# Splits, sums and scans moved from GpSimd to VectorE in a streaming encoder layer

## The chip, the cores and the metric

The kernel runs on one core of a Trainium2 chip. A core has engines that each work through their own queue of instructions in order: TensorE (PE, with its weight loads as PEld), VectorE (DVE), ScalarE (ACT), GpSimd (POOL) and SyncE (SP), which here issues the loads and stores. They wait for each other by semaphores. The metric is device time in microseconds (us); lower is better.

## What is computed

One layer of an encoder for two groups of tokens that share all weights, 512 tokens of a prompt and 32 of a sample (with cached keys, values and states). Everything is float32. Cut to what matters:

```
mod = silu(c) @ w_ada + b_ada;  sh1, sc1, g1, sh2, sc2, g2 = split(mod)
h   = layer_norm(x) * (1 + sc1) + sh1
a_q, a_k, a_v, m_qk, m_v, m_if, m_o = split(h @ w_in)
a_out = differential attention, 4 heads: softmax - lam * softmax, block-causal mask
m_out = mLSTM, 4 heads: conv on q/k, gates, cumulative sum and running maximum over tokens
y_a = head_norm(a_out) @ w_br_a;  y_b = head_norm(m_out) * sigmoid(m_o) @ w_br_b
g_a, g_b = split(sigmoid(h @ w_gate + b_gate))
mix = (g_a * y_a + g_b * y_b) @ w_o
x   = layer_norm(ALPHA * x + (1 + g1) * mix)
h2  = layer_norm(x) * (1 + sc2) + sh2
gt, up = split(h2 @ w_gu);  ffn = (silu(gt) * up) @ w_down
y   = layer_norm(ALPHA * x + (1 + g2) * ffn)
```

## The kernel before

Features lie on the 128 partitions and the 544 tokens on the free axis, in two halves of 256 and 288 tokens. To keep accuracy with TensorE's fast float format, each large product is made of three: every operand is split into a high part (`hi`, `H`: ScalarE's copy into the rounded format) and a low part (`lo`, `L`: the operand minus its high part), and TensorE adds hi x hi, hi x lo and lo x hi. A weight tile is a block of 1024 input rows by 128 columns, held as 128x1024. For each such tile (`Unit`) ScalarE writes `hi`, another engine subtracts and writes `lo`, and TensorE then runs 8 steps of three matmuls for each half of the tokens. `hi`, `lo` and the raw weights `raw` have two buffers each, so a load of new raw weights starts when the last `lo` from that buffer is done, and a `hi` starts when TensorE has left the buffer two tiles back. PSUM banks come from small rings too (tags `g`, `s`, `x`, `o`): a matmul into a reused bank waits for the engine that read it last.

The order is: load and normalise `x`, modulate it into `hH`/`hL` in five stages while the first columns of `w_in` (q and k) are already multiplied (to about 100 us); the rest of `w_in` with attention and mLSTM work laid between its tiles, four groups of columns with the conditioning products between (to about 290 us); the gates; the two branch products, whose results are summed in `br` and split to `mixH`/`mixL` (to about 480 us); `w_o`, the norm and `h2` (to about 580 us); the two feed-forward products (to about 930 us) and the last norm.

Order is set when the program is written out: side work is kept in small generators, and `Lane` emits their steps between the main stream's matmuls, by cost estimates for ScalarE, VectorE and GpSimd. On each engine the emitted order is the order in which it runs.

Who makes the low parts differs by place. Lines as in the profile: `vtt` (L153) is a VectorE operation on two tensors, `gtt` (L157) the same on GpSimd, `sub2` (L159) gives 3 of the 8 slices to GpSimd and 5 to VectorE. `group_split` (L478) uses `gtt` for the first weights, `hunits(..., gtt)` (L1540) for 22 tiles of `w_in`, `sub2` serves `w_o` and the first part of `w_gu`. `scan32` (L908) runs sums on GpSimd and maxima on VectorE. `rsqrt` (L277) always runs on GpSimd.

Of the kernel before, what the change touches and what calls it, by code (L numbers as in the profile page):

```python
# [9 lines left out]
F32 = mybir.dt.float32  # L10
# [9 lines left out]
T = SEQ + DEC  # L20
# [11 lines left out]


class Lane:
    """Emits the steps of generators between the steps of a main stream, by estimates of when each engine gets there."""

    RATE = {"act": (0.2, 0.83e-3), "dve": (0.13, 1.04e-3), "pool": (0.2, 1.8e-3)}
    LAG = 0.15
# [55 lines left out]
def trunk_kernel(ctx: ExitStack, tc: tile.TileContext, I: dict, O: list):  # L94
    nc = tc.nc
# [10 lines left out]
    lane = Lane()  # L106
# [2 lines left out]
        return sp.tile(shape, dt, tag=f"S{i}", name=name)  # L109

    class Halves:
        """Eight tiles of features by tokens, held in the two halves of a slot."""

        def __init__(self, i, dt, name):
            self.h = [slot(f"{i}{c}", [128, 4, T], dt, f"{name}{c}") for c in "ab"]
# [41 lines left out]
        nc.gpsimd.tensor_tensor(out=out, in0=in0, in1=in1, op=op)  # L157
        lane.op("pool", out)

    def sub2(out, in0, in1, op):  # L160
        gtt(out[:, 0:3], in0[:, 0:3], in1[:, 0:3], op)
        c = lane.chain
        lane.begin()
        vtt(out[:, 3:8], in0[:, 3:8], in1[:, 3:8], op)
        lane.chain = max(c, lane.chain)

    def bns(out, in_):
        nc.vector.bn_stats(out=out, in_=in_)  # L168
# [45 lines left out]
    w_in = I["w_in"][0]  # L214
# [127 lines left out]
    ORDER0 = "0p0c1c1wwg0gg21grgr2ghrhhh3hr2r3hr3hrammh"  # L342

    def rows_stats(mv):
        """Mean and variance of the sample's tokens, each held as four rows of a quarter of its features."""
        c = small([128, 4], "rows_c", 2)
        ps = bank("o", "cmb")
        mm(ps[:, 0:2], quart, mv)
        yield ROWS_WAIT
        vcopy(c[:, 0:2], ps[:, 0:2])  # L350
        vtt(c[:, 2:3], mv[:, 0:1], c[:, 0:1], SUB)
        vtt(c[:, 2:3], c[:, 2:3], c[:, 2:3], MUL)
        yield ROWS_WAIT
        mm(ps[:, 2:3], quart, c[:, 2:3])
        yield ROWS_WAIT
        vtt(c[:, 1:2], c[:, 1:2], ps[:, 2:3], ADD)
        return c
# [56 lines left out]
    hH, hL = Halves(0, F32R, "hH"), Halves(1, F32R, "hL")  # L414

    def modulate(k, part=None):
        """Features of tile k: all tokens, or those of one half."""
        t = tmp([128, T], "mod_t")
        cut = (0, T) if part is None else (HALF[part][0], sum(HALF[part]))
        for a, b, r in ((0, 512, 0), (512, 544, 1)):  # L420
            a, b = max(a, cut[0]), min(b, cut[1])
            if a < b:
                vts(t[:, a:b], xT(k)[:, a:b], modT[:, 8 + k, r:r + 1], modT[:, k, r:r + 1], MUL, ADD)
        c = slice(*cut)
        act(hH(k)[:, c], t[:, c], AF.Copy)
        yield 0
        (vtt if part != 0 else gtt)(hL(k)[:, c], t[:, c], hH(k)[:, c].bitcast(F32), SUB)

    def all_of(gen):
        for _ in gen:  # L430
# [50 lines left out]
    def group_split(x):  # L481
        if x in parts or x >= len(groups):
            return
        s, i = groups[x]
        n = STAGES[s]
        r = w_raw[s][:, i]
        hi = wp.tile([128, 2, 512], F32R, tag="hi", name="hi", bufs=2)
        lo = wp.tile([128, 2, 512], F32R, tag="lo", name="lo", bufs=2)
        act(hi[:, 0:n], r, AF.Copy)
        gtt(lo[:, 0:n], r, hi[:, 0:n].bitcast(F32), SUB)  # L490
        parts[x] = (hi, lo)

    qk_holder = {}
# [75 lines left out]
        return hi, lo  # L569

    class Unit:
        """One n-tile of a product: its weights' parts, its matmuls, what takes its results."""

        def __init__(self, chunk, c0, nk, aH, aL, evac, k0=0, ak0=0, halves=(0, 1), split=None, pss=None,
                     first=True, last=True, need=None, eng=None, late=False):
# [33 lines left out]
                    self.evac(ps, hf, o, n)  # L609

    class IfUnit:
        """The gates' eight columns: the weights' two parts side by side, so that each half of h passes once."""

        chunk, need = None, None

# [107 lines left out]


    def to_tok(src, name, tag="x", part=(0, 1)):
        """[128, T] features by tokens into PSUM as tokens by features: the prompt's four tiles, the sample's."""
        out = []
        for i in part:
            p = bank(tag, name + str(i))
            if i == 0:  # L730
                for tt in range(4):
                    tr(p[:, tt * 128:(tt + 1) * 128], src[:, tt * 128:(tt + 1) * 128], 128)
                out.append(p.rearrange("p (t f) -> p t f", t=4))
            else:
                tr(p[0:32, 0:128], src[:, 512:544], 128)
                out.append(p[0:32, 0:128])
        return out
# [168 lines left out]
        return mv[0:32, 4, h, 0:128] if s else mv[:, 0:4, h, 0:128]  # L906

    def scan32(cur, pp, op):  # L908
        big = gtt if op == ADD else vtt
        for i, s in enumerate((1, 2, 4, 8, 16)):  # L910
            nxt = pp[i % 2].rearrange("p (a b) -> p a b", a=17)
            vcopy(nxt[:, :, 0:s], cur[:, :, 0:s])
            big(nxt[:, :, s:32], cur[:, :, s:32], cur[:, :, 0:32 - s], op)
            cur = nxt
            yield 0
        c = small([4, 16], "scan_c")
        vcopy(c.unsqueeze(2), cur[:, 0:16, 31:32])
        for s in (1, 2, 4, 8):
            d = small([4, 16], "scan_d")
            vcopy(d[:, 0:s], c[:, 0:s])  # L920
            vtt(d[:, s:16], c[:, s:16], c[:, 0:16 - s], op)
            c = d
        vtt(cur[:, 1:16, :], cur[:, 1:16, :], c[:, 0:15].unsqueeze(2).to_broadcast([4, 15, 32]), op)
        yield 0
# [612 lines left out]
    units.append(IfUnit())  # L1537

    for c in range(4):
        units += hunits(w_in, 1536 + c * 256, [conv_evac(2 * c), conv_evac(2 * c + 1)], gtt)  # L1540
        units.append(ada_rest.pop(0))
        d = c % 2
        if c < 2:
            units += hunits(w_in, 2560 + d * 256, [v_evac(2 * d, mv_dst, None), v_evac(2 * d + 1, mv_dst, None)], gtt)
        else:
            units += hunits(w_in, 3080 + d * 256, [og_evac(2 * d), og_evac(2 * d + 1)], gtt)
        units.append(ada_rest.pop(0))

    tas = []
# [34 lines left out]
    def br_b_evac(n):  # L1584
        def f(ps, hf, o, w):
            if not mix:
                mix["H"], mix["L"] = Halves(0, F32R, "mixH"), Halves(1, F32R, "mixL")
            p = tmp([128, 288], "br")[:, 0:w]
            stt(p, tas[1](n)[:, o:o + w], 1.0, ps[:, 0:w], ADD, MUL)
            gtt(p, p, tas[0](n)[:, o:o + w], ADD)  # L1590
            dH, dL = mix["H"](n)[:, o:o + w], mix["L"](n)[:, o:o + w]

            def g():
                act(dH, p, AF.Copy)
                yield 0
                vtt(dL, p, dH.bitcast(F32), SUB)
            mix_tasks.append(lane.add(g()))
        return f
# [152 lines left out]
    def h2_parts(tf, H, L, i):  # L1751
        lane.begin()
        act(H, tf, AF.Copy)
        yield 0
        (gtt if i in POOL_LO else vtt)(L, tf, H.bitcast(F32), SUB)

    def mod2(out, in_, kk, r, eng):
        sc, sh = modT[:, 32 + kk, r:r + 1], modT[:, 24 + kk, r:r + 1]
# [76 lines left out]
            )  # L1835

    SLACK, ROWS_LATE = 2.5, 0.0
    MODE = ((0, 1), (0, 1), (2, 1), (0, 1))
    ACT_MOD = ((0, 2), (0, 1, 3))
    POOL_LO = ((0, 1), (1, 1))  # L1840
    ACT_POOL = ((0, 0), (1, 0))

    wo = {}

# [16 lines left out]
    def split_to(raw, where):  # L1861
        hi, lo = part_pair(where)
        act(hi, raw, AF.Copy)
        sub2(lo, raw, hi.bitcast(F32), SUB)
        return hi, lo

    wo_parts = {}
# [46 lines left out]
    def u_evac(n):  # L1914
        def f(ps, hf, o, w):
# [4 lines left out]
            def g():  # L1920
                act(dH, th, AF.Copy)
                yield 0
                (gtt if (n, hf) in ACT_POOL else vtt)(dL, th, dH.bitcast(F32), SUB)
            act_tasks.append((n, lane.add(g())))
        return f

# [184 lines left out]
```

## Time and profile before

| what | value |
|---|---|
| median of 3 runs | 963.54 us (962.74 to 964.62) |
| profiled execution, first to last instruction | 966.0 us, 2.5 above the median of the runs |
| mean granted TensorE clock of the profiled execution | 0.982 |
| TensorE busy | 916.9 us, 95% |
| VectorE busy | 525.4 us, 54%, 1113 instructions |
| ScalarE busy | 355.8 us, 37% |
| GpSimd busy | 214.1 us, 22%, 253 instructions |
| GpSimd, full `lo` of `w_in` tiles | 20 of 2415 ns |
| VectorE, full `lo` | 72 of 1224 ns |

All times after the third row are of the profiled execution, and places are given in us from its start. A row of the timeline has start, length, engine, line, operation, output<-inputs and shape, and in brackets how long the engine had been idle and what ended that. The releaser is inferred from semaphores.

### The profile page before, as it was taken

To read this page: it belongs to the slowest core of one execution; us is meant where nothing else is said; L and a number is where in the kernel's file an instruction comes from. 1 tells how busy PE (TensorE), PEld (TensorE's weight loads), DVE (VectorE), ACT (ScalarE), POOL (GpSimd) and SP (SyncE) were. 2 spreads that over 40 slices of the span, in tenths; PEclk is the share of its full clock that TensorE was granted. 3 is DMA by queue.
4 is the path that set the end of the run, shared out by engine and by line. 5 is a ranking of instruction groups with operands and counts; after the bars stand their busy time and mean duration, and the time that the engine had idled before them with its cause. 6 is when DMAs were issued, how large, how long until landed. Compare 5 with 4: busy or idle time off the path is not lost. (4 is left out here: it accounts for less than half of the span.)

```text
span 966.0 us, 17335 instructions
## 1 busy us (share of the span) xinstructions
PE 916.9 (95%) x7184; PEld 868.2 (90%) x7184; DVE 525.4 (54%) x1113; ACT 355.8 (37%) x689; POOL 214.1 (22%) x253
## 2 busy tenths in 40 slices
PE   4799999999999999999999989999999999999993
PEld 4679998798798889899999989999999999999993
DVE  4657567877554444446846886544444443223356
ACT  4511466555542332322434474322222222212241
POOL 4433116332411100101741664200000000000014
PEclk8989999999999999999999999999999999999997
DMA  9904423252244244333911502022222226322302
GB/s 281 337 1 127 147 67 112 88 174 89 88 132 143 93 141 133 93 132 124 309 63 45 192 32 89 1 88 88 89 88 88 88 88 232 123 77 77 121 1 92
DMA packets 92283, 110.43 MB, mean 114 GB/s; under 512 B 3897, under 2 KB 75789, under 8 KB 92205
## 3 DMA queue, kind: packets, MB, share of 16 engines
q1 hardware_dynamic: 91996, 109.27, 34.8%
q8 instruction: 56, 0.92, 0.4%
q14 instruction: 23, 0.18, 0.1%
q10 hardware_dynamic: 208, 0.07, 0.0%
HBM read 102.09 MB, written 7.24 MB: 113 GB/s over the span
## 5 line engine op out<-in xcount | busy, mean ns | idle before, releaser
L153 DVE TENSOR_TENSOR lo<-raw,hi 128x1024 fp32r<-128x1024 f32 (+3 forms) x102 | 112.0, 1098 | 130.4 <-ACT hi L132 125.4
L132 ACT ACTIVATE hi<-raw 128x1024 fp32r<-128x1024 f32 (+2 forms) x124 | 122.1, 984 | 153.1 <-PE dn L600 61.6
L600 PE MATMUL dn<-act,hi 128*128 128x288 f32 (+1 forms) x704 | 135.8, 292 | 0.0
L600 PE MATMUL g<-hHa,hi 128*128 128x288 f32 (+1 forms) x344 | 109.1, 317 | 6.2 <-DVE qka L176 4.7
L600 PEld LDWEIGHTS dn<-act,hi 128*128 128x128 f32 x704 | 110.8, 189 | 0.0
L600 PE MATMUL g<-hHb,hi 128*128 128x256 f32 (+1 forms) x352 | 107.8, 306 | 1.3 <-DVE qka L176 1.3
L600 PE MATMUL g<-h2Ha,lo 128*128 128x288 f32 (+1 forms) x352 | 101.4, 288 | 2.4 <-POOL lo L157 1.5
L600 PE MATMUL dn<-act,lo 128*128 128x288 f32 (+1 forms) x352 | 101.8, 289 | 1.8 <-DVE lo L153 1.8
L600 PE MATMUL g<-h2La,hi 128*128 128x288 f32 (+1 forms) x352 | 101.4, 288 | 1.0 <-DVE h2La L153 1.0
L600 PE MATMUL g<-h2Ha,hi 128*128 128x288 f32 (+1 forms) x352 | 102.1, 290 | 0.0
L600 PE MATMUL g<-hLb,hi 128*128 128x256 f32 (+1 forms) x352 | 101.9, 289 | 0.0
L600 PE MATMUL g<-hLa,hi 128*128 128x288 f32 (+1 forms) x344 | 101.2, 294 | 0.8 <-DVE hLa L153 0.7
L600 PE MATMUL g<-h2Hb,hi 128*128 128x288 f32 (+1 forms) x352 | 101.8, 289 | 0.0
L600 PE MATMUL g<-h2Lb,hi 128*128 128x288 f32 (+1 forms) x352 | 101.5, 288 | 0.1
L600 PE MATMUL g<-hHb,lo 128*128 128x256 f32 (+1 forms) x352 | 101.4, 288 | 0.0
L600 PE MATMUL g<-hHa,lo 128*128 128x288 f32 (+1 forms) x344 | 100.7, 293 | 0.2 <-DVE lo L153 0.2
L600 PE MATMUL g<-h2Hb,lo 128*128 128x288 f32 (+1 forms) x352 | 100.8, 286 | 0.0
L157 POOL TENSOR_TENSOR lo<-raw,hi 128x1024 fp32r<-128x1024 f32 (+2 forms) x30 | 63.6, 2122 | 137.1 <-ACT hi L132 126.5
L600 PEld LDWEIGHTS g<-hHa,hi 128*128 128x128 f32 x344 | 66.0, 192 | 23.0 <-issue 6.2
L280 POOL TENSOR_SCALAR rs__10439<-mv__10423 128x1 f32<-128x1 f32 x1 | 0.2, 190 | 322.4 <-DVE mv__10423 L172 322.4
L600 PEld LDWEIGHTS g<-hHb,hi 128*128 128x128 f32 x352 | 66.7, 190 | 5.3 <-issue 2.7
L600 PEld LDWEIGHTS g<-h2Ha,lo 128*128 128x128 f32 x352 | 66.3, 188 | 3.1 <-POOL lo L157 2.0
(490 smaller groups left out, 2180.4 us busy)
## 6 DMA issues: line engine op xcount, KB each, us to landing
raw<-in_w_gu_dram SPq DMA_DIRECT2D x18, 1024.0 KB, 5.1
raw<-in_w_ada_dram SPq DMA_DIRECT2D x16, 1024.0 KB, 5.2
raw<-in_w_in_dram SPq DMA_DIRECT2D x10, 1024.0 KB
raw<-in_w_gate_dram SPq DMA_DIRECT2D x8, 1024.0 KB, 6.7
raw<-in_w_down_dram SPq DMA_DIRECT2D x8, 1024.0 KB, 5.3
wo<-in_w_o_dram SPq DMA_DIRECT2D x4, 1024.0 KB
rawg<-in_w_gu_dram SPq DMA_DIRECT2D x4, 1024.0 KB
raw<-in_w_down_dram SPq DMA_DIRECT2D x3, 768.0 KB
```

What stands on the lines that cost most here:

```text
L132: nc.scalar.activation(out=out, in_=in_, func=func, **kw)
L153: nc.vector.tensor_tensor(out=out, in0=in0, in1=in1, op=op)
L157: nc.gpsimd.tensor_tensor(out=out, in0=in0, in1=in1, op=op)
L280: nc.gpsimd.tensor_scalar(out=out, in0=in_, scalar1=scale, scalar2=EPS, op0=MUL, op1=ADD)
L600: nc.tensor.matmul(ps[:, 0:n], w[:, self.k0 + k, :], a(self.ak0 + k)[:, o:o + n], start=(self.first and k == 0 and p == 0), stop=(self.las ...
```

## The change

Every split that was on GpSimd, wholly or in part, goes to VectorE; so do the sums of the two branches (`br`) and the additions of the scans. A new helper `ltt` is a VectorE operation that still books its time as GpSimd's in `Lane`, so that most of the emitted order stays as it was; where `vtt` is used instead, the booking changes too. In the norm after `w_o`, token tile 2 is now computed by two VectorE passes like the other tiles, where it had one pass on ScalarE, one on VectorE and one on GpSimd. GpSimd keeps the inverse roots, masks, constants and small copies.

```diff
-    def sub2(out, in0, in1, op):
-        gtt(out[:, 0:3], in0[:, 0:3], in1[:, 0:3], op)
-        c = lane.chain
-        lane.begin()
-        vtt(out[:, 3:8], in0[:, 3:8], in1[:, 3:8], op)
-        lane.chain = max(c, lane.chain)
+    def ltt(out, in0, in1, op):
+
+        nc.vector.tensor_tensor(out=out, in0=in0, in1=in1, op=op)
+        lane.op("pool", out)
...
     def modulate(k, part=None):
-        (vtt if part != 0 else gtt)(hL(k)[:, c], t[:, c], hH(k)[:, c].bitcast(F32), SUB)
+        vtt(hL(k)[:, c], t[:, c], hH(k)[:, c].bitcast(F32), SUB)
...
     def group_split(x):
-        gtt(lo[:, 0:n], r, hi[:, 0:n].bitcast(F32), SUB)
+        ltt(lo[:, 0:n], r, hi[:, 0:n].bitcast(F32), SUB)
...
     def scan32(cur, pp, op):
-        big = gtt if op == ADD else vtt
+        big = ltt if op == ADD else vtt
...
-        units += hunits(w_in, 1536 + c * 256, [conv_evac(2 * c), conv_evac(2 * c + 1)], gtt)
+        units += hunits(w_in, 1536 + c * 256, [conv_evac(2 * c), conv_evac(2 * c + 1)], ltt)
...
     def br_b_evac(n):
-            gtt(p, p, tas[0](n)[:, o:o + w], ADD)
+            ltt(p, p, tas[0](n)[:, o:o + w], ADD)
...
     def h2_parts(tf, H, L, i):
-        (gtt if i in POOL_LO else vtt)(L, tf, H.bitcast(F32), SUB)
+        vtt(L, tf, H.bitcast(F32), SUB)
...
-    MODE = ((0, 1), (0, 1), (2, 1), (0, 1))
+    MODE = ((0, 1), (0, 1), (0, 1), (0, 1))
-    POOL_LO = ((0, 1), (1, 1))
-    ACT_POOL = ((0, 0), (1, 0))
...
     def split_to(raw, where):
-        sub2(lo, raw, hi.bitcast(F32), SUB)
+        vtt(lo, raw, hi.bitcast(F32), SUB)
...
-                (gtt if (n, hf) in ACT_POOL else vtt)(dL, th, dH.bitcast(F32), SUB)
+                vtt(dL, th, dH.bitcast(F32), SUB)
```

The edit is made the same way on the other `hunits(..., gtt)` lines. Three places show what it does to the queues. The first is VectorE's queue around 33 us: `mod_t` and `hLa` are the modulated tile and its low part, `s_a` a buffer of raw weights. Before:

```order
L149 TENSOR_SCALAR mod_t<-xTa,modT 128x512
L149 TENSOR_SCALAR mod_t<-xTa,modT 128x32
L153 TENSOR_TENSOR hLa<-mod_t,hHa 128x544
L176 SCALAR_TENSOR_TENSOR qkb<-g,qkb 128x256 x3
L180 COPY gs<-ga 128x512
```

Now:

```order
L149 TENSOR_SCALAR mod_t<-xTa,modT 128x512
L149 TENSOR_SCALAR mod_t<-xTa,modT 128x32
L162 TENSOR_TENSOR lo<-s_a,hi 128x512
L153 TENSOR_TENSOR hLa<-mod_t,hHa 128x544
L174 SCALAR_TENSOR_TENSOR qkb<-g,qkb 128x256 x3
L178 COPY gs<-ga 128x512
L174 SCALAR_TENSOR_TENSOR qkb<-g,qkb 128x256
L162 TENSOR_TENSOR lo<-s_a,hi 128x1024
```

A `lo` stands ahead of `hLa`, and another ahead of the next `qka`; before, both were in GpSimd's queue. The second place is TensorE's queue at about 182 us, with what each row waits for (`v_tok` and `gt` are transposes into banks of the same ring, `gt` of the conditioning sums `ada_gs`). Before:

```order
L600 MATMUL g<-hHa,lo 128x256
L142 MATMUL v_tok_2204<-ident,vT 32x128 [waits DVE_49]
L142 MATMUL gt<-ident,ada_gs 128x128 [waits DVE_49]
L142 MATMUL gt<-ident,ada_gs 128x128 x3
L600 MATMUL g<-hHb,hi 128x256
```

Now:

```order
L598 MATMUL g<-hHa,lo 128x256
L142 MATMUL v_tok_2204<-ident,vT 32x128 [waits DVE_49]
L142 MATMUL gt<-ident,ada_gs 128x128 [waits Activation_49]
L142 MATMUL gt<-ident,ada_gs 128x128 x3
L598 MATMUL g<-hHb,hi 128x256
```

The rows are the same, but `gt` is given another bank of its ring and waits for ScalarE in place of VectorE: for `wT`, ScalarE's copy of transposed attention weights. At about 218 us VectorE's queue changes as in the first place: a `lo` comes in ahead of `colT`, which copies transposed mLSTM rows out of PSUM. The third is VectorE's queue near 578 us, at the last pieces of `h2` (`128x4x32` is the sample's part). Before:

```order
L153 TENSOR_TENSOR h2La<-h2t,h2Ha 128x2x256
L153 TENSOR_TENSOR h2Lb<-h2t,h2Hb 128x2x256
L176 SCALAR_TENSOR_TENSOR th<-th,g 128x256
L153 TENSOR_TENSOR lo<-raw,hi 128x640
L153 TENSOR_TENSOR h2La<-h2t,h2Ha 128x4x32
L153 TENSOR_TENSOR h2Lb<-h2t,h2Hb 128x2x256
```

Now:

```order
L153 TENSOR_TENSOR h2Lb<-h2t,h2Hb 128x2x256
L153 TENSOR_TENSOR th<-th,g 128x256
L153 TENSOR_TENSOR lo<-raw,hi 128x1024
L153 TENSOR_TENSOR h2Lb<-h2t,h2Hb 128x2x256
L153 TENSOR_TENSOR act_6716<-th,act_6715 128x256
L153 TENSOR_TENSOR h2La<-h2t,h2Ha 128x4x32
L153 TENSOR_TENSOR h2Lb<-h2t,h2Hb 128x4x32
```

The `lo` ahead of the sample's `h2La` is now that of the next tile, and two more rows stand between.

More of the change, by code (lines that the diff above doesn't have):

```diff
@@ L1543, in trunk_kernel @@
         if c < 2:
-            units += hunits(w_in, 2560 + d * 256, [v_evac(2 * d, mv_dst, None), v_evac(2 * d + 1, mv_dst, None)], gtt)
+            units += hunits(w_in, 2560 + d * 256, [v_evac(2 * d, mv_dst, None), v_evac(2 * d + 1, mv_dst, None)], ltt)
         else:
-            units += hunits(w_in, 3080 + d * 256, [og_evac(2 * d), og_evac(2 * d + 1)], gtt)
+            units += hunits(w_in, 3080 + d * 256, [og_evac(2 * d), og_evac(2 * d + 1)], ltt)
         units.append(ada_rest.pop(0))
```

## The prediction

> **What bounds the kernel now.** I read the engine totals first, then the table of stretches, then the list of what TensorE waited for.
>
> ```profile
> PE 916.9 (95%) x7184; PEld 868.2 (90%) x7184; DVE 525.4 (54%) x1113; ACT 355.8 (37%) x689; POOL 214.1 (22%) x253
> ```
>
> TensorE is busy for 95% of the span, VectorE for 54%, GpSimd for 22%. So work that moves between the two costs nothing by its sum; it costs or gains only where TensorE waits. In the stretches below the columns are the length, then busy time of PE, PEld, DVE, ACT and POOL with their counts, the granted clock, the DMA share and GB/s.
>
> ```profile
> 48.00:52.00 4.00, 3.32 (x13) 2.88 (x13) 2.20 (x3) 1.29 (x2) 4.00 (x3) 0.50 0.00 2
> ...
> 156.00:160.00 4.00, 4.00 (x21) 3.84 (x22) 3.87 (x10) 1.21 (x5) 0.71 (x1) 0.63 0.56 195
> ...
> 624.00:912.00 288.00, 288.00 (x2300) 288.00 (x2298) 105.51 (x162) 78.81 (x128) 0.00 (x0) 1.00 0.32 104
> ```
>
> From 624 to 912 us TensorE never pauses and GpSimd has no instruction: the change moves nothing there. What it moves lies ahead of 624 us, apart from an untouched tail. The first two rows show something a busy share hides: a few us after a stall the clock fell to 0.50 and 0.63, so a stall can cost more than its length. TensorE's waits (us in total, times, longest):
>
> ```profile
> PE g L600 <- DVE qka L176: 6.0, 3, 3.5
> ...
> PE s_ps L1111 <- DVE mx L992: 1.6, 2, 1.5
> ...
> PE g L600 <- POOL lo L157: 1.5, 1, 1.5
> ...
> PE wT_ps L142 <- DVE ada_gs L153: 1.2, 1, 1.2
> ...
> PE o_ps L136 <- ACT wT L132: 1.1, 1, 1.1
> ...
> PE g L600 <- DVE h2La L153: 1.0, 1, 1.0
> ...
> PE ps_wc L136 <- DVE s_m L180: 0.9, 1, 0.9
> ```
>
> These sum to 13.3 us, and all but the o_ps one end on VectorE or GpSimd. They are most of what the change can win; what it can lose is not in this list, because those waits don't exist yet.
>
> **The price of the moved work.** The groups by form give both engines' times for one operation (count, then busy us and mean ns of one).
>
> ```profile
> L157 POOL TENSOR_TENSOR lo<-raw,hi 128x1024 fp32r<-128x1024 f32 x20 | 48.3, 2415 | 121.4 <-ACT hi L132 111.7 <-ACT lsum L132 9.1 <-DVE s_g L180 0.5
> ...
> L157 POOL TENSOR_TENSOR lo<-rawg,hi 128x384 fp32r<-128x384 f32 x16 | 24.0, 1503 | 19.1 <-ACT hi L132 19.1
> ...
> L157 POOL TENSOR_TENSOR br<-br,ta0a 128x288 f32<-128x288 f32 x4 | 5.1, 1272 | 2.9 <-ACT hi L132 2.0 <-DVE br L176 0.8
> ...
> L153 DVE TENSOR_TENSOR lo<-raw,hi 128x1024 fp32r<-128x1024 f32 x72 | 88.2, 1224 | 95.0 <-ACT hi L132 91.1 <-PE qk_ps L136 3.7
> ...
> L153 DVE TENSOR_TENSOR lo<-rawg,hi 128x640 fp32r<-128x640 f32 x16 | 15.2, 951 | 5.3 <-ACT hi L132 5.3
> ```
>
> A full `lo` takes 2.42 us on GpSimd and 1.22 us on VectorE. The 22 full ones cost VectorE 22 x 1.22 = 27 us; the 32 that it shared go from 640 to 1024 elements, 32 x (1.22 - 0.95) = 9 us or a little more; the 16 `br` sums and the scans add some 10 by the same rate. That is 45 to 55 us more asked of VectorE. Tile 2's normalisation adds one pass over 1024 elements and takes one from ScalarE. All of this is costed at nothing by its length, because TensorE's own work covers it wherever VectorE has idle time; what it costs without that cover is the third rival. VectorE also gets time back, since operations of its own that meet a GpSimd tensor operation take far longer than their size:
>
> ```profile
> 42.05 3.99 DVE L149 TENSOR_SCALAR mod_t<-xTa,modT 128x512 f32<-128x512 f32 x4
> ...
> 42.06 2.35 POOL L157 TENSOR_TENSOR lo<-s_a,hi 128x1024 fp32r<-128x1024 f32 x1
> ```
>
> Two pieces of 512 and two of 32 elements took 3.99 us, 2.35 of them beside the `lo`. [...]
>
> The GpSimd `lo` row shows the other side: it idled 121.4 us before those twenty, 111.7 of it until ScalarE's `hi` was there. GpSimd could afford to stand and wait. VectorE is a queue as well, and now that `lo` stands in it; everything listed behind waits for the same `hi`. So each term below is this (rows of the timeline: start, length, engine, line, operation, in brackets the idle time before and what ended it): when is `hi` ready, plus 1.22 us, plus what stands between, against when TensorE took the result before.
>
> **First stage, 33 to 52 us.**
>
> ```profile
> 33.02 0.72 DVE L153 TENSOR_TENSOR hLa<-mod_t,hHa 128x544 fp32r<-128x544 f32 x1 [0.72 <-ACT hHa L132]
> ...
> 33.77 0.64 ACT L132 ACTIVATE hi<-s_a 128x512 fp32r<-128x512 f32 x1
> ...
> 33.80 0.39 PE L600 MATMUL g<-hLa,hi 128*128 128x256 f32 x1
> ...
> 47.82 1.96 DVE L153 TENSOR_TENSOR hLa<-mod_t,hHa 128x544 fp32r<-128x544 f32 x2
> ...
> 48.24 1.05 ACT L132 ACTIVATE hi<-s_a 128x1024 fp32r<-128x1024 f32 x1
> ...
> 48.59 0.58 PE L600 MATMUL g<-hLa,hi 128*128 128x256 f32 x1 [0.45 <-DVE hLa L153]
> ```
>
> TensorE took `hLa` at 33.80 us, right when it was done. Now a 512 `lo` precedes it, and its `hi` ends at 33.77 + 0.64 = 34.41. With 0.72 us for the `lo` (the 544-element row bounds it) and 0.72 for `hLa`, TensorE goes on at 35.9: **+2.1 us**. Next comes the 3.5 us wait for `qka` at 42.67 to 46.42 us. [...] Then `hLa` again: `hi` ends at 49.29, `lo` at 50.5, `hLa` (half of 1.96, or 0.72) near 51.3 instead of 48.59: **+2.7**.
>
> **142 to 156 us.**
>
> ```profile
> 144.14 0.62 DVE L176 SCALAR_TENSOR_TENSOR s_att<-s_att,r 128x384 f32<-128x384 f32 x1
> ...
> 144.54 1.06 ACT L132 ACTIVATE hi<-raw 128x1024 fp32r<-128x1024 f32 x1 [0.54 <-DMA raw<-in_w_in_dram]
> ...
> 147.20 0.49 PE L142 MATMUL wT_ps<-ident,s_att 128*128 128x128 f32 x3
> ...
> 150.50 5.07 DVE L176 SCALAR_TENSOR_TENSOR cv_y<-cv_u,PT,cv_y 128x547 f32<-128x547 f32 x3
> ```
>
> `s_att` now stands behind that `lo` (ready 145.60, done 146.8) and three `s_g` rows that are no longer than 0.62 each by estimate: done between 147.5 and 149.3 against TensorE's 147.20, so +0.3 to +2.1, I take +1.5. [...]
>
> **182 to 187 us.** Here a wait changes its owner. `gt` got a PSUM bank that VectorE's `s_m` copy released; now it gets the one that ScalarE's `wT` releases (the order rows of TensorE ahead of this text show it).
>
> ```profile
> 178.37 0.37 SPq L184 DMA_DIRECT2D raw<-in_w_in_dram  x1
> ...
> 182.77 0.66 PE L142 MATMUL gt<-ident,ada_gs 128*128 128x128 f32 x4 [0.42 <-DVE s_m L180]
> ...
> 185.17 1.06 ACT L132 ACTIVATE hi<-raw 128x1024 fp32r<-128x1024 f32 x1 [4.17 <-DMA raw<-in_w_in_dram]
> ...
> 186.13 0.47 ACT L132 ACTIVATE wT<-wT_ps 128x384 f32<-128x384 f32 x1
> ```
>
> `wT` waits behind a `hi` that waits for a load, and that load was issued when GpSimd's `lo` left the buffer. VectorE's `lo` leaves it 2.42 - 1.22 = 1.2 us earlier, so `wT` ends at 186.60 - 1.2 = 185.4 and `gt` starts at 185.5 instead of 182.77: +2.7. The o_ps wait of 1.1 for that `wT` is then paid already: **+1.6** (if TensorE were not bound there, -1.1).
>
> **218 us.**
>
> ```profile
> 211.58 0.37 SPq L184 DMA_DIRECT2D raw<-in_w_in_dram  x1
> ...
> 218.41 0.28 PE L142 MATMUL v_tok<-ident,vT 128*32 128x128 f32 x1 [0.21 <-DVE colT L180]
> ...
> 218.78 1.06 ACT L132 ACTIVATE hi<-raw 128x1024 fp32r<-128x1024 f32 x1 [2.53 <-DMA raw<-in_w_in_dram]
> ```
>
> The load takes 7.2 us from issue to `hi`, and comes 0.6 us earlier. `hi` ends at 219.2, `lo` at 220.5, and only then `colT` frees the bank that `v_tok` needs: 220.7 against 218.41, +2.3, less the 0.9 wait of ps_wc just behind: **+1.4**.
>
> **Later places.** [...] The wait for GpSimd's own `lo` at 547 us goes: **-1.5**. Then 578 us:
>
> ```profile
> 578.60 1.06 ACT L132 ACTIVATE hi<-raw 128x1024 fp32r<-128x1024 f32 x1 [1.26 <-issue]
> ...
> 579.62 0.68 DVE L153 TENSOR_TENSOR h2Lb<-h2t,h2Hb 128x512 fp32r<-128x512 f32 x1
> ...
> 579.75 0.40 PE L600 MATMUL g<-h2La,hi 128*128 128x288 f32 x1 [0.99 <-DVE h2La L153]
> ```
>
> That `hi` reuses a buffer which TensorE's unit releases at 578.6, so it cannot come sooner. Before, `h2La`'s rows stood ahead of its `lo`; now they stand behind it, `h2Lb` and one `act`. So 579.66 + 1.22 + 0.68 + about 0.45 for a 256-element `act` and 0.25 for the rows (both estimated from the 0.68 of 512) = 582.3, and TensorE stands 3.7 us instead of 1.0: **+2.7**.
>
> Sum: 2.1 - 1.5 + 2.7 + 0 + 1.6 + 1.4 - 1.0 - 1.5 + 2.7 = **+6.5 us**. The profiled execution spans 966.0, so it would be 972.5; the median of the runs shown is 963.54, 2.5 below, so I forecast **970**. Smaller places of either sign, each under 1 us, are left to the range. So is the clock: a stretch at lower speed costs (1 - 0.63) x 4 = 1.5 us by the second row of stretches, and I let those that come with new stalls and those that go with old ones cancel, with two either way (3 us). The terms' own bounds add about 5, so its own range is 964 to 977. [...]
>
> **Rivals.** [...]
>
> *No change.* The two signs cancel: the five prices at half, 10.5 / 2 = 5.2, against -4.0 in the three gains and one clock stretch less: 963 to 965. For it: each price assumes that TensorE has no other wait to absorb it. Against: all five lie where TensorE took the result within 0.1 us of its end, or waited for it.
>
> *Much slower.* VectorE becomes the bound where it is nearly full:
>
> ```profile
> 450.00:480.00 30.00, 30.00 (x240) 29.77 (x239) 24.13 (x51) 13.78 (x28) 15.98 (x16) 1.00 0.83 279
> ...
> 552.00:576.00 24.00, 21.78 (x174) 20.41 (x173) 21.29 (x41) 16.06 (x27) 16.01 (x18) 1.00 0.13 50
> ```
>
> In the second stretch it has 2.7 us free of 24, and each shared `lo` grows by 0.27: 32 x 0.27 = 9 us over all such places if none is hidden, giving 979. [...]
>
> That the work is not moved at all is excluded: the order rows show the `lo` in VectorE's queue.
>
> **How the numbers follow.** About 0.2%, or 2 us, is what a measurement here can tell from no change. Forecast 0.50 and much slower 0.10 make slower 0.60; no change 0.16; faster 0.24. The range of 957 to 978 leaves out about one in ten at each end.
>
> **What would show it.** Right: `hLa` near 35.9 and 51.3 with TensorE behind it, `gt` waiting for ScalarE's `wT` near 183, `v_tok` waiting for `colT` 2 us at 218, `h2La` a wait of over 3 us near 580, no `qka` wait over 2.5, none on GpSimd's `lo`, `mod_t` near 1.6 us for the four; VectorE between 525 and 560 us busy. Wrong: the positive waits missing from TensorE's list (then faster), or VectorE over 90% busy from 528 to 576 with TensorE waiting for each `lo` (then much slower). A change in 624 to 912 us would refute the whole frame.

## The result, and the profile after

The changed kernel takes 976.62 us (median of four runs, 971.34 to 977.46) against 963.14 us for the kernel before beside it: a ratio of 1.0129, 95% interval 1.0101 to 1.0158. It is slower, 6.6 us above the forecast of 970 and inside the range of 957 to 978. Measured once more on another occasion it gave 972.44 us, ratio 1.0093 (1.0069 to 1.0117).

The engine totals of the changed kernel, from the page of its profiled run (span 969.6 us, time 971.34 us):

```profile
PE 914.5 (94%) x7184; PEld 867.7 (89%) x7184; DVE 527.8 (54%) x1166; ACT 354.4 (37%) x688; POOL 76.7 (8%) x167
```

GpSimd lost 137 us of work and VectorE gained 53 instructions, yet VectorE's busy time rose by 2.4 us only (525.4 to 527.8), where the prediction counted 45 to 55 us of new work. So about that much of VectorE's old busy time had been spent waiting beside GpSimd, inside its own instructions: the lengths of the 959 VectorE rows whose operation, names, form and count are the same in both profiles sum to 416 us before and 371 now. The change did return that time. It did not help, because over the span VectorE is not the bound (it is busy for 54% of it, and only near 580 us does TensorE stand for more than 2 us while VectorE has no pause, as shown below); the waits of TensorE moved. What it waits for now (us in total, times, longest):

```profile
PE g L598 <- DVE hLa L153: 5.3, 2, 3.2
PE g L598 <- DVE h2La L153: 4.3, 1, 4.3
PE v_tok L142 <- DVE colT L178: 3.5, 1, 3.5
PE g L598 <- DVE qka L174: 3.3, 6, 1.6
...
PE gt L142 <- ACT wT L132: 1.6, 1, 1.6
...
PE wT_ps L142 <- DVE s_att L174: 1.3, 1, 1.3
```

The waits for GpSimd's `lo`, for `mx` and for `ada_gs` are gone, and `qka` fell from 6.0 to 3.3. In their place stand `hLa`, `h2La`, `colT`, `wT` and `s_att`, all of them places that the prediction named. The rows of three of them (start, length, engine, line, operation, in brackets the idle time before and what ended it):

```profile
32.26 0.64 ACT L132 ACTIVATE hi<-s_a 128x512 fp32r<-128x512 f32 x1
32.93 0.69 DVE L162 TENSOR_TENSOR lo<-s_a,hi 128x512 fp32r<-128x512 f32 x1 [2.14 <-ACT hi L132]
33.54 0.72 DVE L153 TENSOR_TENSOR hLa<-mod_t,hHa 128x544 fp32r<-128x544 f32 x1
34.31 0.39 PE L598 MATMUL g<-hLa,hi 128*128 128x256 f32 x1 [2.09 <-DVE hLa L153]
...
48.18 1.05 ACT L132 ACTIVATE hi<-s_a 128x1024 fp32r<-128x1024 f32 x1
49.26 1.23 DVE L162 TENSOR_TENSOR lo<-s_a,hi 128x1024 fp32r<-128x1024 f32 x1 [1.42 <-ACT hi L132]
50.40 1.35 DVE L153 TENSOR_TENSOR hLa<-mod_t,hHa 128x544 fp32r<-128x544 f32 x2
51.17 0.58 PE L598 MATMUL g<-hLa,hi 128*128 128x256 f32 x1 [3.21 <-DVE hLa L153]
...
577.77 1.22 DVE L153 TENSOR_TENSOR lo<-raw,hi 128x1024 fp32r<-128x1024 f32 x1
...
580.45 1.22 DVE L153 TENSOR_TENSOR lo<-raw,hi 128x1024 fp32r<-128x1024 f32 x1
...
582.52 0.28 DVE L153 TENSOR_TENSOR h2La<-h2t,h2Ha 128x128 fp32r<-128x128 f32 x1
...
582.86 0.61 PE L598 MATMUL g<-h2La,hi 128*128 128x288 f32 x1 [4.31 <-DVE h2La L153]
```

Each time VectorE stands idle until ScalarE's `hi` is there (2.14 and 1.42 us in brackets), does the `lo`, and only then the rows that TensorE is waiting for. Near 580 two weight splits of 1.22 us and some smaller rows stand ahead of one of 0.28 us.

The stretches around that last stall, of the changed kernel (length, busy time of PE, PEld, DVE, ACT and POOL, granted clock, DMA share, GB/s):

```profile
578.00:580.00 2.00, 0.49 (x2) 0.19 (x1) 2.00 (x3) 1.33 (x3) 0.00 (x0) 1.00 0.00 0
580.00:583.00 3.00, 0.14 (x1) 0.14 (x1) 3.00 (x8) 0.42 (x1) 0.00 (x0) 0.66 0.00 0
583.00:585.00 2.00, 2.00 (x9) 2.00 (x10) 0.34 (x2) 0.00 (x0) 0.00 (x0) 0.50 0.04 8
585.00:587.00 2.00, 2.00 (x10) 2.00 (x10) 0.00 (x0) 0.00 (x0) 0.00 (x0) 0.50 0.00 0
```

Behind the stall TensorE does 9 or 10 matmuls in 2 us instead of 17 or 18: the clock is at a half for some 5 us, and matmuls start another 1.8 us later by the end of it. This is the part of the result that the prediction did not carry.

### The profile page after: what moved, and what is told of

It reads as the page before. It is cut to its first block, busy times and chain, and to the rows that moved or that the text cites. A ratio compares the mean times of both kernels' runs of the same rounds, so it can differ in the third digit from the quotient of the medians.

```text
span 969.6 us, 17226 instructions
## 1 busy us (share of the span) xinstructions
PE 914.5 (94%) x7184; PEld 867.7 (89%) x7184; DVE 527.8 (54%) x1166; ACT 354.4 (37%) x688; POOL 76.7 (8%) x167
## 5 line engine op out<-in xcount | busy, mean ns | idle before, releaser
L153 DVE TENSOR_TENSOR lo<-raw,hi 128x1024 fp32r<-128x1024 f32 (+2 forms) x102 | 114.7, 1124 | 127.5 <-ACT hi L132 123.0
L598 PEld LDWEIGHTS g<-hLa,hi 128*128 128x128 f32 x344 | 65.9, 192 | 6.2 <-DVE hLa L153 5.7
L598 PEld LDWEIGHTS g<-h2La,hi 128*128 128x128 f32 x352 | 66.7, 189 | 4.5 <-DVE h2La L153 4.5
```

The lines of the kernel that those rows point to most:

```text
L153: nc.vector.tensor_tensor(out=out, in0=in0, in1=in1, op=op)
L598: nc.tensor.matmul(ps[:, 0:n], w[:, self.k0 + k, :], a(self.ak0 + k)[:, o:o + n], start=(self.first and k == 0 and p == 0), stop=(self.las ...
```

## The experiments

All were timed in five rounds beside the kernel before, whose median was 962.9 to 964.9 us on all occasions. "Place" means how much later the same matmul starts than in the profile named. One table for all; the last two columns are means over the timed runs, from the span and granted clock of each: span x (1 - clock), the time given up to a lowered clock (a stall inside such a stretch is counted in it), and span x clock, the rest. The clock is given to three digits, so one run is good to about 0.5 us and the spread within a kernel is 1 to 2.

| kernel | median us | ratio to before | span x (1 - clock) | span x clock |
|---|---|---|---|---|
| before (beside the repeat) | 963.92 | 1 | 13.9 | 948.8 |
| change, first occasion | 976.62 | 1.0129 (1.0101 to 1.0158) | 21.9 | 951.9 |
| change, repeated | 972.44 | 1.0093 (1.0069 to 1.0117) | 20.7 | 951.1 |
| start's splits back | 968.13 | 1.0050 (1.0029 to 1.0071) | 19.3 | 948.0 |
| 16 w_in tiles back | 966.33 | 1.0031 (1.0013 to 1.0049) | 15.2 | 950.2 |
| w_o and feed-forward back | 967.65 | 1.0046 (1.0031 to 1.0062) | 13.6 | 952.9 |
| sample's h2La on GpSimd | 967.70 | 1.0036 (1.0020 to 1.0053) | 16.3 | 950.2 |
| h2La ahead in the queue | 970.74 | 1.0055 (1.0034 to 1.0077) | 18.1 | 949.9 |
| TensorE filled in the stall | 970.74 | 1.0063 (1.0032 to 1.0094) | 17.0 | 952.2 |
| only the seven splits moved | 982.78 | 1.0179 (1.0156 to 1.0202) | 22.7 | 957.8 |
| only sums, scans, norm moved | 966.87 | 1.0023 (1.0009 to 1.0037) | 14.8 | 950.6 |
| combined | 954.64 | 0.9898 (0.9872 to 0.9925) | 11.6 | 941.6 |
| combined, repeated | 953.71 | 0.9878 (0.9859 to 0.9898) | 8.6 | 943.2 |
| combined, norm back | 957.24 | 0.9940 (0.9920 to 0.9960) | 10.5 | 944.8 |

The kernel before has 948.5 to 948.8 in the last column on every occasion, so the column can be compared across them.

**The change once more.** Expected were 966 to 969 us if the places were the whole loss, 974 to 978 if this kernel always draws a lower clock, and runs spread over both if the lower clock goes with the execution. The median of 972.44 us lies between the first two. The runs of both occasions spread from 971.3 to 978.2 us, so the third fits best, though none is as low as 969.

**One group back at a time.** The theory on trial: the loss comes from a few splits that stand in VectorE's in-order queue ahead of what TensorE waits for. Its rivals: the loss comes with the amount of VectorE work, or with the clock.

```diff
 # start's splits back (undo_start)
-        vtt(hL(k)[:, c], t[:, c], hH(k)[:, c].bitcast(F32), SUB)
+        (vtt if part != 0 else gtt)(hL(k)[:, c], t[:, c], hH(k)[:, c].bitcast(F32), SUB)
-        ltt(lo[:, 0:n], r, hi[:, 0:n].bitcast(F32), SUB)
+        gtt(lo[:, 0:n], r, hi[:, 0:n].bitcast(F32), SUB)
 # 16 w_in tiles back (undo_hunits): ltt -> gtt in the three hunits(w_in, ...) calls
 # w_o and feed-forward back (undo_ffn): sub2, POOL_LO, ACT_POOL and MODE as before
```

> The changed kernel with the low parts of the first ten weight splits (up to about 86 us) and of the first modulated tile back on GpSimd; the rest as changed. Queue theory (each place costs what stands in VectorE's queue there): the waits for hLa at 34 and 51 us (2.0 + 2.7) and for k_tok at 86 us (1.0) go, and the gains of that stretch go too (about 1.9 at the start, 0.6 net at 42 to 46 us, 1.9 at 64 and 80 us): 1 to 2 us faster than the changed kernel. Sum theory (time follows the amount of work moved): ten of the 22 full splits, a fifth of all moved work, 2 to 3 us faster. Clock theory (most of the 13 us is half-speed stretches that follow stalls): up to 5 us faster, with a higher granted clock in 24 to 72 us.

> The changed kernel with the sixteen low parts of the later w_in tiles (120 to 275 us) back on GpSimd; the rest as changed. Queue theory: the waits at 123, 147, 183 and 218 to 222 us (0.5 + 1.6 + 1.3 + 3.4) go, and the gains at 154, 187, 223 and 249 us (1.5 + 1.0 + 1.1 + 1.4) go too, with one half-speed stretch either way: 2 us faster than the changed kernel, 1 to 5. Sum theory: 16 of 22 full splits, about a third of the moved work, 4 us faster. The wait of gt for wT at 183 us is expected to be gone from TensorE's list.

> The changed kernel with everything from w_o on as before (shared splits, two h2 pieces, two act pieces and tile 2's normalisation on GpSimd and ScalarE); starts, w_in tiles, scans and br sums as changed. Queue theory: the wait for h2La near 580 us falls from 4.3 to 1.0 us and its half-speed stretch (1.6) goes, but the 3.5 us won from 528 to 574 us and 0.9 at 480 us are given back: within 1 us of the changed kernel. Sum theory: the 32 shared splits and the rest are almost half the moved work, 5 to 6 us faster.

Against the profile of the change, the places came back one by one. Start: the matmuls at 34 and 51 us are 2.0 and 2.65 us earlier and the one at 87 us 0.95, while those from 66 and from 82 us on come about 0.45 later each. w_in tiles: `s_att` at 151 us 1.53 earlier, `gt` 1.25 (its wait for `wT` is gone, as expected), `v_tok` at 223 us 3.34, while the rows near 158, 228 and 255 us lose 0.81, 1.06 and 1.34 again. Feed-forward: `h2La` 3.41 earlier, and 3.24 lost on the way to it from 488 us. So every group holds a loss and a gain, each at its own place; all three gave a ratio well under the change's. They don't add up: 0.4 to 0.6% each against the repeat's 0.93%, and undoing all three together (below) leaves 0.23%. By ratio they are some 4, 6 and 4.5 us faster than the repeat, where the queue theory had 1 to 2, about 2 and at most 1, and the sum theory 2 to 3, 4 and 5 to 6: on the whole time neither has the sizes. The last column tells them apart. Against the repeat it changes by -3.1, -0.9 and +1.8 us, which is within about 2 us of the queue theory each time and the reverse of the sum theory's order, by which the last group, almost half of the moved work, should have given back most. The clock column has the rest (-1.4, -5.5 and -7.1). Each of the three puts GpSimd work back in the way of VectorE, so each pays a part of its win again. For the w_in tiles that can be seen in the three `cv_y` rows beside GpSimd's `lo`: 4.42 us against 2.42 in the change; before they took 5.07 us. First the change, then the kernel with the w_in tiles back:

```profile
155.12 2.42 DVE L174 SCALAR_TENSOR_TENSOR cv_y<-cv_u,PT,cv_y 128x547 f32<-128x547 f32 x3
```

```profile
152.87 4.42 DVE L174 SCALAR_TENSOR_TENSOR cv_y<-cv_u,PT,cv_y 128x547 f32<-128x547 f32 x3
153.25 2.62 POOL L157 TENSOR_TENSOR lo<-raw,hi 128x1024 fp32r<-128x1024 f32 x1 [1.53 <-issue]
```

**One 128x128 split to GpSimd.** VectorE is kept, but the sample's `h2La`, the last thing in its queue near 580 us, goes to the empty GpSimd.

```diff
+    def dgt(out, in0, in1, op):
+        nc.gpsimd.tensor_tensor(out=out, in0=in0, in1=in1, op=op)
+        lane.op("dve", out)
-        vtt(L, tf, H.bitcast(F32), SUB)
+        (dgt if i == (2, 0) else vtt)(L, tf, H.bitcast(F32), SUB)
```

> The changed kernel with one single instruction of 128x128 elements, the sample's h2La near 580 us, on GpSimd instead of VectorE, planned as if it were on VectorE so that the written order stays. Queue theory: it no longer stands behind a split, one h2Lb and one act, so TensorE's 4.3 us wait for it falls below 1 us and the half-speed stretch behind it (1.6 us) goes: 3.5 to 5 us faster than the changed kernel. Sum theory: 0.1 us of work moved, no change.

```profile
578.72 2.33 POOL L166 TENSOR_TENSOR h2La<-h2t,h2Ha 128x128 fp32r<-128x128 f32 x1 [8.53 <-ACT h2Ha L132]
...
581.09 0.40 PE L602 MATMUL g<-h2La,hi 128*128 128x288 f32 x1 [2.01 <-POOL h2La L166]
```

The stall fell from 4.31 to 2.01 us, not below 1 as expected, and 3.4 us at half speed still follow it. The small operation took 2.33 us, where three GpSimd operations of 128x288 take 2.30 together at 47 us in the profile of the change (additions for q and k, which the change left on GpSimd). VectorE had no pause from 578.30 to 581.05 us. By this row the waiting goes both ways, and the empty GpSimd queue beside a full VectorE was not a quick way out here.

**The order in the queue.** The engine stays VectorE; only the step that lets other work go between `h2Ha` and `h2La` of the sample is left out.

```diff
-        yield 0
+        if i != (2, 0):
+            yield 0
```

> The change with one thing moved: VectorE issues the 128 x 4 x 32 split of the sample's h2 ahead of the weight splits that stood before it; nothing changes its engine. Queue theory (the 4.3 us wait near 580 is VectorE's queue, not the time of the operation): the wait falls below 1.5 us, the half-speed stretch behind it (1.6 us) goes, 3.5 to 5 us less than the change beside it. Work theory (VectorE is full there, 3 us of work must be waited for anyway): the wait moves to the next weight split, a wait on lo of 2 to 4 us stands there, and at most 1 us is gained.

From the waits of TensorE:

```profile
PE g L598 <- DVE h2Lb L153: 1.3, 1, 1.3
...
PE g L598 <- DVE h2La L153: 1.3, 1, 1.3
```

One wait of 4.3 us became two of 1.3, no half-speed stretch follows, and the matmuls from 588 us on have gained 3.5 us against the change. The work theory's 2 to 4 us wait for the next weight split is not there. So 1.7 us of that stall and the half-speed stretch behind it were order. The 2.6 us that stay are not: VectorE works without a pause there from 579.6 to 588 us. The whole kernel takes 970.74 against 972.44 us, with overlapping intervals: one place of several.

**The clock by itself.** The stall is kept, and TensorE is given something to do in it: 14 matmuls whose result is overwritten.

```diff
+                for _ in range(self.fill):      # 14 for the first sample-half unit, else 0
+                    nc.tensor.matmul(
+                        ps[:, 0:n], hi[:, self.k0, :], self.aH(self.ak0)[:, o:o + n], start=True, stop=True,
+                    )
                 for k in range(self.nk):
```

> The change with 14 matmuls more, whose result is overwritten, ahead of the first sample-half matmul of the feed-forward, so that TensorE works while it would wait for the 4.3 us of h2La near 580. The arithmetic that counts is the same. 14 x 0.24 us = 3.4 us of work go into the wait. Clock theory (a wait of some 4 us costs a half-speed stretch behind it): the wait shows as under 1.2 us, the granted clock stays 1.00 from 582 to 588, and 1.4 to 1.8 us are gained there. Without it (the stretch falls where it will): a stretch of 3 to 4 us at half speed stands there all the same, and nothing is gained, or up to 0.5 us lost.

The stretches and the stalled matmul of this kernel:

```profile
583.00:585.00 2.00, 0.28 (x3) 0.04 (x1) 2.00 (x4) 0.42 (x1) 0.00 (x0) 1.00 0.00 0
585.00:587.00 2.00, 1.29 (x9) 1.29 (x10) 1.19 (x5) 0.00 (x0) 0.00 (x0) 1.00 0.00 0
587.00:589.00 2.00, 2.00 (x17) 2.00 (x16) 0.00 (x0) 0.00 (x0) 0.00 (x0) 1.00 0.00 0
```

```profile
581.03 2.12 PE L598 MATMUL g<-h2Ha,hi 128*128 128x288 f32 x14
...
585.71 0.40 PE L603 MATMUL g<-h2La,hi 128*128 128x288 f32 x1 [2.42 <-DVE h2La L153]
```

The half-speed stretch is gone, and matmuls gain 2.2 us between 583 and 588 us against the change, with the same arithmetic and more work. My size was off: the 0.24 us was read from rows at half speed, and the 14 took 2.12 us, so 2.42 us of idle were left instead of under 1.2. Even so the clock held. In one profile a stretch could be absent by chance; over all the profiles it goes with the stall here. The four with an `h2La` wait of 4.3 us (the change, its repeat, start's splits back, the w_in tiles back) lose 1.7 or 3.4 us to the clock at 578 to 594 us, those with 3.1 and 2.0 us (small things only, one split on GpSimd) lose 1.7 each, and those with 1.0 to 1.3 us (before, feed-forward back, order, the seven splits, the combined ones) nothing. The filled one, with 2.4 us idle behind work, loses nothing either. Elsewhere idle times of 2.4 us (548 us, small things only) and 2.6 us (219 us, w_o and feed-forward back) brought no stretch, so it is not shown whether the work in the gap kept the clock up or only the shorter idle behind it. Its runs against the repeat's (970.74 to 972.44 us) overlap, so the gain is shown at its place only.

**Prices without gains.** The kernel before, with only seven splits moved: those with x = 3, 5 and 9 of the start and four of the w_in tiles.

```diff
-        gtt(lo[:, 0:n], r, hi[:, 0:n].bitcast(F32), SUB)
+        (ltt if x in (3, 5, 9) else gtt)(lo[:, 0:n], r, hi[:, 0:n].bitcast(F32), SUB)
 # in hunits, with the GpSimd tiles counted by seq:
+                if seq[0] in (0, 2, 6, 10):
+                    eng_ = ltt
```

> The kernel before with only seven of the moved splits on VectorE: those of the start whose x is 3, 5 and 9, and four of the sixteen w_in tiles (the 1st, 3rd, 7th and 11th). These are the seven that the combined kernel keeps on GpSimd; all else as before, so GpSimd still holds 214 - 17 us of work less these seven. Queue theory (the loss comes from a few splits that stand in VectorE's queue ahead of what TensorE waits for, place by place): their places lose 2.0 + 2.6 + 1.0 + 0.5 + 1.6 + 1.3 + 3.4 = 12 us, less 1.0 and 1.0 of waits paid already behind the last two; with no gain against it, slower than the change itself: 971 to 977 us, ratio 1.008 to 1.014. Amount theory (the loss comes with the 45 us more that VectorE is asked for): 17 us of 45 moved, under half of the change's loss: 964 to 968 us, ratio 1.001 to 1.005.

```profile
PE g L605 <- DVE qka L181: 6.0, 3, 3.5
PE g L605 <- DVE hLa L153: 5.3, 2, 3.2
PE gt L142 <- ACT wT L132: 4.1, 1, 4.1
PE v_tok L142 <- DVE colT L185: 2.7, 1, 2.7
PE wT_ps L142 <- DVE s_att L181: 2.2, 1, 2.2
```

The strongest run of the study: a fraction of the moved work makes the kernel 1.79% slower, more than all of it did. The amount theory (at most 1.005) is out; the queue theory has the sign, but its range (to 1.014) was too low. The new waits of the change stand here beside the old `qka` wait. Against before the places are +2.0 (34 us), +2.8 (48), +1.0 (86), +0.6 (121), +2.5 (147), +3.7 - 1.0 (183 to 187), +2.6 - 0.8 (218 to 223): some 13 us against the 10 I expected net, the excess at `s_att` and `gt`, and in the table 8.4 us go to the clock (a stall inside a half-speed stretch counts in both figures, so they don't add up).

**Gains without prices.** The seven stay on GpSimd, everything else moves, and the sample's `h2La` goes ahead in the queue.

```diff
-        ltt(lo[:, 0:n], r, hi[:, 0:n].bitcast(F32), SUB)
+        (gtt if x in (3, 5, 9) else ltt)(lo[:, 0:n], r, hi[:, 0:n].bitcast(F32), SUB)
 # in hunits, with the VectorE tiles counted by seq:
+                if seq[0] in (0, 2, 6, 10):
+                    eng_ = gtt
 # and the yield of h2_parts left out for i == (2, 0)
```

> On GpSimd again: the first, second and last of the start's splits that hold matmuls up, and four of the sixteen w_in tiles; the sample rows' split of the feed-forward's input stays on VectorE but is not made to yield its turn; all else as in the change. Work theory: the places sum to 2.0 + 2.6 + 1.0 + 0.5 + 1.6 + 3.4 + 3.4 us given back with the gains of the change (64, 80, 121, 251, 488 to 574: about 7 us) kept, so faster than before: 953 to 959 us, ratio 0.990 to 0.996. Rival (the gains hang on GpSimd being empty, and come back as waits on GpSimd's lo once it has work): 962 to 966 us, ratio 0.999 to 1.003.

> The combined kernel once more, on another occasion. If its gain belongs to the kernel: ratio 0.987 to 0.993, as before. If a part of it was the granted clock of that occasion (0.984 to 0.993 over its runs against 0.984 to 0.990 of the kernel before): ratio 0.993 to 0.997.

The page of the first of the two:

```profile
PE 911.5 (96%) x7184; PEld 865.2 (91%) x7184; DVE 524.8 (55%) x1159; ACT 354.1 (37%) x688; POOL 93.2 (10%) x174
```

954.64 and 953.71 us, ratios 0.9898 and 0.9878: about 1.1% faster than before and 2% faster than the change, with 16.5 us of GpSimd work between the change and it. The first ratio lies at the fast end of the expected 0.990 to 0.996, the second inside its range, so the gain belongs to the kernel. In the table 6 to 7 us of it are waits and work, and 2 to 6 us are the clock, which in both profiles is not lowered once between 52 and 940 us. This kernel beats both.

**Only the small things.** All splits as before; the br sums, the scans' additions and one tile's normalisation moved ("norm" in the table).

```diff
 # all splits into parts as in the kernel before; kept from the change:
+        big = ltt if op == ADD else vtt
+            ltt(p, p, tas[0](n)[:, o:o + w], ADD)
+    MODE = ((0, 1), (0, 1), (0, 1), (0, 1))
```

> The change without its splits: every split into high and low parts where it was before, and only the four br sums' additions, the scans' additions and the second normalisation step of one tile moved to VectorE. Queue theory: none of the places of the loss is touched, and the gains that came with GpSimd's empty queue (64, 80, 156, 251, 528 to 574 us) are not there either; only the wait near 483 us shrinks, by up to 0.9: 961 to 965 us, ratio 0.998 to 1.002. Rival (the scans and sums bear a part of the price): 966 to 970 us, ratio 1.002 to 1.007.

```profile
PE g L605 <- DVE h2La L153: 3.1, 1, 3.1
PE g L605 <- POOL lo L157: 2.8, 2, 2.4
```

A ratio of 1.0023 (1.0009 to 1.0037), at the border of what both expected. TensorE starts 2.4 us later at 552 us and 2.1 later at 580. I took the normalisation step for the cause and gave it back in the combined kernel:

```diff
-    MODE = ((0, 1), (0, 1), (0, 1), (0, 1))
+    MODE = ((0, 1), (0, 1), (2, 1), (0, 1))
```

> The combined kernel with one part more taken back: the normalisation of the prompt's third tile of 128 tokens again by a ScalarE pass, a multiplication on VectorE and an addition on GpSimd. In the run that moved only the sums, scans and this step, TensorE came 2.4 us later at 552 us and 2.1 us later at 580. If that step is the cause: the waits of 1.3 and 1.3 us for h2La and h2Lb near 568 us shrink together below 1.5 us, and 1 to 2.5 us are gained against the combined kernel: 951.5 to 953.5 us, ratio 0.985 to 0.988. If the splits of the feed-forward in that queue are the cause, or the step is covered: no difference against it, ratio 0.987 to 0.991; if its GpSimd addition of 1024 elements meets VectorE's split, a loss of 1 to 2 us.

```profile
537.84 3.07 POOL L157 TENSOR_TENSOR u_t<-u_t,s_u 128x1024 f32<-128x1024 f32 x1
...
538.58 3.42 DVE L178 SCALAR_TENSOR_TENSOR u_t<-u_t,rs__6396,s_u 128x1024 f32<-128x1024 f32 x1
```

The loss of the last clause, and more of it than expected: a ratio of 0.9940 against 0.9898 and 0.9878. GpSimd's addition of 3.07 us holds up a VectorE row of another tile (3.42 us, where another such row of this profile takes 1.28, at 534.71 us), and from 528 to 564 us TensorE does 265 matmuls instead of the 286 in the combined kernel's second profile. There the move to VectorE was a gain. Why the same move cost about 2 us beside GpSimd's feed-forward splits stays open.

## Why the prediction was right, and where it was not

Its sign and range held, and most of its terms did. Place by place, in the two profiles of before and change:

| place (us) | predicted | measured |
|---|---|---|
| 33.8 `hLa` | +2.1 | +2.0 |
| 42 `qka` | -1.5 | -0.6 |
| 48.6 `hLa` | +2.7 | +2.65 |
| 147 `s_att`, 156 `s_ps` | +1.5, -1.5 | +1.6, -1.5 |
| 182 `gt`, 187 `o_ps` | +2.7, -1.1 | +1.25, -1.0 |
| 218 `v_tok`, 223 `ps_wc` | +2.3, -0.9 | +3.4, -1.05 |
| 249 `ada_gs` | -1.0 | -1.35 |
| 488 to 574, GpSimd's `lo` among it | -1.5 | -3.55 |
| 578 `h2La` | +2.7 | +3.4 |
| sum | +6.5 | +5.2 |

Three terms, -1.5 at `qka`, 0 for `s_att` and `s_ps` together and -1.0 at `ada_gs`, were my estimates of what VectorE's time beside GpSimd's `lo` is worth to TensorE when it comes back, and no run shows them at these sizes; the two profiles show -0.6, +0.1 and -1.35 there, with the four `mod_t` pieces at 1.42 us instead of 3.99 and the three `cv_y` rows at 2.42 instead of 5.07.

**The queue terms were right in kind and nearly in size**, and two runs show that they are the cause: seven splits alone, put into VectorE's queue, make the kernel before 1.8% slower; with the same seven left on GpSimd and the sample's `h2La` ahead in the queue, the rest of the change makes it 1.1% faster. *Right in kind, mis-sized:* `gt` and `v_tok` hang on a load. The rows of the change (SPq is the issue):

```profile
176.88 0.37 SPq L182 DMA_DIRECT2D raw<-in_w_in_dram  x1
...
182.24 1.06 ACT L132 ACTIVATE hi<-raw 128x1024 fp32r<-128x1024 f32 x1 [1.52 <-DMA raw<-in_w_in_dram]
183.20 0.47 ACT L132 ACTIVATE wT<-wT_ps 128x384 f32<-128x384 f32 x1
...
183.73 0.66 PE L142 MATMUL gt<-ident,ada_gs 128*128 128x128 f32 x4 [1.65 <-ACT wT L132]
...
212.02 0.37 SPq L182 DMA_DIRECT2D raw<-in_w_in_dram  x1
...
220.33 1.06 ACT L132 ACTIVATE hi<-raw 128x1024 fp32r<-128x1024 f32 x1 [3.48 <-DMA raw<-in_w_in_dram]
221.42 1.23 DVE L162 TENSOR_TENSOR lo<-raw,hi 128x1024 fp32r<-128x1024 f32 x1 [7.86 <-ACT hi L132]
222.56 0.29 DVE L178 COPY colT<-R_tok 128x64 f32<-128x64 f32 x2
...
222.83 0.39 PE L142 MATMUL v_tok<-ident,vT 128*32 128x128 f32 x1 [3.46 <-DVE colT L178]
```

The chain is the predicted one. The first load took 5.4 us from issue to `hi` instead of before's 6.8, the second 8.3 instead of 7.2, and both differences went one for one into the stall. In the repeat the first took 6.9 us, and `gt` came 2.7 us late, the term as predicted:

```profile
186.46 1.06 ACT L132 ACTIVATE hi<-raw 128x1024 fp32r<-128x1024 f32 x1 [3.08 <-DMA raw<-in_w_in_dram]
...
187.95 1.11 PE L142 MATMUL gt<-ident,ada_gs 128*128 128x128 f32 x4 [3.21 <-ACT wT L132]
```

At 580 us the estimate let the last `lo` start when its `hi` was done; VectorE came to it only at 580.45, with rows of its own still ahead, and that is the 0.7 us.

**The gains were undersized.** For 547 us one listed wait of 1.5 us was taken; the stretch to 574 us gave 3.55. The same holds at 64 and 80 us, left out as small, where TensorE gained 0.45 us each (a wait of 1.25 us for `qka` before, two short ones now), because the VectorE pair of `hLb` rows took 2.67 us beside GpSimd's `lo` before and 1.35 now:

```profile
64.67 1.35 DVE L153 TENSOR_TENSOR hLb<-mod_t,hHb 128x544 fp32r<-128x544 f32 x2
```

```profile
61.54 2.39 POOL L157 TENSOR_TENSOR lo<-raw,hi 128x1024 fp32r<-128x1024 f32 x1 [8.78 <-ACT hi L132]
...
62.49 2.67 DVE L153 TENSOR_TENSOR hLb<-mod_t,hHb 128x544 fp32r<-128x544 f32 x2
```

Smaller places of the other sign (`k_tok` at 86 us +0.96, 121 us +0.53, 245 us +0.5) outweigh these two by about 1 us, so with them the places come close to the predicted sum.

**The step that failed is the clock**, put as "I let those that come with new stalls and those that go with old ones cancel, with two either way (3 us)". Over the runs of the repeat the change has 20.7 us of clock loss against before's 13.9, 6.8 us more. Not all of this is slower work, since a stall inside a half-speed stretch counts by half: in the repeat's profile TensorE stands still for 18.7 of 55.3 us at half speed, in before's for 12.6 of 34.2, so 3 of the 10.5 us of clock loss between these two are stall. By difference, what the places leave of the medians is 8.5 - 5.2 = 3 us in the repeat and 13.5 - 5.2 = 8 us on the first occasion; this is an estimate of the clock's share. The pair of profiles above hides it: the change has 37.1 us at half speed there against 34.2, only 1.5 us more lost, so the profiles differ by 3.6 us and the medians by 8.5 and 13.5.

In the profiles, the losses between 24 and 940 us come in steps of 1.7 us, which is 3.4 us at half speed; the change's profile has 7 such steps, the repeat's 10, before's 4, the combined kernel's 3 and 1. The new stalls of the change's profile are 1.3 to 4.3 us long, and five of the six are followed by one or two steps. The length does not settle it: the 1.3 us at `s_att` and the two idle times named with the filled kernel (2.4 and 2.6 us) have no stretch behind them, 1.5 us at 154 us in the profile of before has one, and one and the same kernel has ten steps in one execution and seven in another. What decides it is not shown here. At 578 us, where the prediction took the stall's length alone, half speed cost 1.8 us more.

So the forecast of 970 was made of a sum that was 1.3 too high at its places (less with the unlisted ones) and a clock term that was too low by some 3 us in the repeat and 8 on the first occasion. That it lies no further off is in part luck: the misses at the places (-1.45 at `gt`, +1.1 at `v_tok`, -2 from 488 to 574 us) partly cancel, and what is left of them has the other sign than the clock's miss.

**The rivals.** *Faster* (chance 0.24): the change is slower on both occasions, 1.0129 and 1.0093, and all five prices stood. But the time VectorE gets back, 44 us by the rows of equal form, is what the combined kernel lives on. *No change*: excluded by both intervals. *Much slower, VectorE the bound* (979): the stretch in question, 488 to 574 us, became 3.55 us shorter. Just behind it, from 578 to 583 us, VectorE is full (5.00 of 5 us) while TensorE stands (0.63 busy).

## What to carry to other kernels

When work moves between two in-order queues, its busy time says little; ask of each moved instruction what it waits for and what stands behind it. A split that waits for a load or a late producer belongs on the queue where nobody is waiting, even at twice its length (2.42 against 1.22 us for a full `lo`), and the rest on the other: here seven of more than fifty cost 1.8% between them when they stood in the wrong one. Price a new stall by its length plus the half-speed stretch behind it (1.7 or 3.4 us lost around the 4.3 us stall here), from several runs and not from one profile, and look whether TensorE has something harmless to do meanwhile (shown here at one place of one profile).

## What was not expected of the hardware

- VectorE's busy time stayed at 525 to 528 us, the low end of the 525 to 560 predicted, with some 45 us of work added, since rows beside GpSimd's tensor operations had been counted as busy while held up (`hLb` 2.67 against 1.35 us, `cv_y` 5.07 against 2.42). GpSimd seems to be held up likewise: 2.33 us for one 128x128, against 2.30 for three 128x288.
- Run to run, the time of one kernel follows the granted clock: before's span x clock is 948.8 us with a standard deviation of 0.9 over 17 runs, while their spans go from 959.9 to 965.3 us.
- The same transfer into `raw` near 180 and 212 us took between 5.1 and 8.5 us from issue to use over the profiles, and TensorE saw all of the difference between before and the change: -1.4 us at `gt` and +1.1 at `v_tok`.
- With 2.1 us of throwaway matmuls in a stall of 4.3 us the clock stayed up behind it, in the one profile of that kernel; the four profiles with the bare stall all lost 1.7 or 3.4 us there.
